# Mixer weights ahead in priority, the mLSTM gate rows and the output gate as later threads: a float32 trunk of two layers

## The chip, the cores and the metric

The kernel runs on one core of a Trainium2 chip. The metric is the device time of one execution in microseconds (us); lower is better.

## The reference

The program is a streaming-encoder trunk with two layers, 512 frames and 1024 channels, all in float32. Each layer adds half a SwiGLU feed-forward block, then a mixer block, then half a SwiGLU block again. The mixer block reads one normalised input through one projection whose columns are shared out among an RWKV-7 mixer, an mLSTM mixer and two merge gates:

```python
xn = _rmsnorm(h, mix_norm[l])
z = xn @ w_in[l]                                  # all columns of both mixers and of the gates
r, k, v, xw, xa, xg = _split_cols(shifted z_rw)   # RWKV-7: 8 heads of 64
...
g = jax.nn.sigmoid(xg) @ g_up                     # RWKV-7's output gate
y_a = ((y + bonus) * g)
y_b = _mlstm_mixer(mq, mk, mv, mo, mi, mf, ...)   # 4 heads of 128, input and forget gate rows mi, mf
u = sigmoid(g_a) * (y_a @ br_a[l]) + sigmoid(g_b) * (y_b @ br_b[l])
h = h + u @ w_out[l]
```

In layer 1 the RWKV value is mixed with that of layer 0 through a low-rank gate (`xn @ vres_down`, then `vres_up`).

## The kernel before, in words

Activations lie transposed, channels on partitions and the 512 frames along the free axis. To keep float32 accuracy every large product is made of three: weights and activations are split into a high part rounded to float32r and a low part that is the rest, and TensorE multiplies high by high, high by low and low by high (`product`, lines 460 to 462). A projection job has 128 output columns and eight steps of 128 input channels, so 24 matmuls. Its weights (512 KB) are loaded by `weights`: one DMA on the SyncE queue into `wraw` (two buffers), then for each half a rounding cast on ScalarE into `whi` (line 424) and a subtraction on VectorE into `wlo` (line 425). `whi` and `wlo` have four half-buffers each, so the splits can be two jobs ahead of TensorE, and no more.

The order of TensorE's work in the mixers is written out by a planner, `Weave`. Each piece of the mixers is a Python generator, a thread with a rank. A thread yields what it waits for: a planned time (`at`), a flag that another thread sets (with a planned time), a lock, or a projection job (`proj`). The planner keeps a planned TensorE time `t` and a planned VectorE time `dve` (`mark`, `pe`); when a thread is ready it runs on, lowest rank first; otherwise TensorE gets the next step of the current job, and a new job goes to the waiting thread of lowest rank. If nobody is ready and nobody waits for a job, the planned time jumps ahead. `manual_schedule` fixes this order for TensorE alone.

The other engines are ordered by the tile framework: each engine's queue is written at build time by going through a planned run and taking, among the instructions that are ready, the one with the lowest priority number. Priority numbers count up in the order in which the program issues instructions. On the chip each queue then runs in that fixed order.

The threads are `common` (rank -1: the jobs `misc`, `wa`, `xg`), four `rwkv` threads (ranks 0 to 3, jobs `k`, `r`, `v` of two heads each, then a chunked recurrence), the mLSTM heads (8), the mLSTM projections (9), the mLSTM gate rows (10) and, as filler, the sixteen merge-gate jobs (`gates_spilled`, 20). Job `misc` carries the mLSTM input and forget gate rows, 32 columns of `xg` and the low-rank value columns. In the kernel before, the gate rows begin when `misc` is shifted (flag `misc`), the jobs follow each other as `misc`, `wa`, `xg`, and `xg` is shifted, passed through a sigmoid and made ready inside `common`, which sets the flag `common`. The RWKV threads begin at the flag `wa`, with the two matmuls of lines 923 and 927 that read `wa`.

Of the kernel before, what the change touches and what calls it, by code (L numbers as in the profile page):

```python
# [12 lines left out]
F32R = mybir.dt.float32r  # L13
AF = mybir.ActivationFunctionType
ALU = mybir.AluOpType
# [215 lines left out]
class Weave:  # L231
# [48 lines left out]
    def run(self):  # L280
        trunk = self.trunk
        job = None
        self.threads.sort(key=lambda th: th[0])
        while job or any(not th[3] for th in self.threads):
            th = next((th for th in self.threads if self.ready(th[2])), None)
            if th is not None:
                if th[2][0] == "lock":
                    self.held.add(th[2][1])
                self.resume(th)
                continue  # L290
            if job is None:
                th = next((th for th in self.threads if th[2][0] == "proj"), None)
                if th is not None:
                    job = [th, trunk.weights(th[2][1]), trunk.mm(), 0]
                    th[2] = ("job", None)
                    self.mark(0.0, 1.4)
            if job is not None:
                th, w, ps, k = job
                trunk.product(ps, w, k, trunk.xh[:, k, :], trunk.xl[:, k, :], k == 0, k == KD - 1)
                self.t += self.STEP + (0.1 if self.small else 0.0)  # L300
                self.small = False
                job[3] += 1
                if job[3] == KD:
                    job = None
                    self.resume(th, ps)
                continue
            times = [th[2][1] for th in self.threads if th[2][0] == "at"]
            times += [self.flags[th[2][1]] for th in self.threads if th[2][0] == "flag" and th[2][1] in self.flags]
            self.t = min(times)
# [19 lines left out]
class Trunk:  # L329
# [246 lines left out]
    def mixers(self, l, done):  # L576
        nc = self.nc
        self.l = l
        self.src = {n: self.a["wi"][l, i] for i, n in enumerate(WIN_TILES)}
        src = self.src  # L580
# [21 lines left out]
        wv.add(-1, self.common())  # L602
        for p in range(4):
            wv.add(p, self.rwkv(p))
        wv.add(8, self.mlstm_heads())
        wv.add(9, self.mlstm_projections())
        wv.add(10, self.mlstm_gates())
# [24 lines left out]
        for i in range(KD):  # L632
            w = self.weights(self.a["br"][l, i])
            for j in (1, 0):
                g = gates[i][j]
                ps = self.mm()
# [23 lines left out]
        self.wv.mark(1.4, 0.7)  # L660

    def gates_spilled(self, early):
        yield "flag", "rows"
        for i in range(16):
            ps = yield "proj", self.src[f"g{'ab'[i % 2]}{i // 2}"]
            g = self.tmp(f"t{1 + i % 2}", 1)
            self.gate(ps, g)
            self.nc.sync.dma_start(out=self.gd[i], in_=g)
            early.add(i)
# [21 lines left out]
    def mlstm_gates(self):  # L691

        nc, l, zm, wv = self.nc, self.l, self.zm, self.wv
        yield "flag", "misc"
        rc, gem = self.tmp("t2", 1), self.m_gem
        slab, rt, ru = self.tmp("t1", 1), self.tmp("t0"), self.tmp("t0")
        ifb = self.col(l, "ifb")
        F = slice(64, 68)
        I = slice(32, 36)
        nc.gpsimd.memset(slab, 0.0)  # L700

        nc.vector.tensor_scalar(out=rt[F], in0=zm[F], scalar1=ifb[F], scalar2=None, op0=ALU.add)
        nc.scalar.activation(out=ru[F], in_=rt[F], func=AF.Abs)
        nc.scalar.activation(out=ru[F], in_=ru[F], func=AF.Exp, scale=-1.0)
        nc.scalar.activation(out=ru[F], in_=ru[F], func=AF.Ln, bias=1.0)
        nc.vector.tensor_scalar(out=rt[F], in0=rt[F], scalar1=-1.0, scalar2=0.0, op0=ALU.mult, op1=ALU.max)
        nc.vector.tensor_tensor(out=rt[F], in0=rt[F], in1=ru[F], op=ALU.add)
        nc.vector.tensor_tensor_scan(out=ru[F], data0=rt[F], data1=rt[F], initial=0.0, op0=ALU.add, op1=ALU.bypass)
        nc.vector.tensor_copy(out=rt[I], in_=ru[F])
        nc.vector.scalar_tensor_tensor(out=slab[I], in0=zm[I], scalar=ifb[I], in1=rt[I], op0=ALU.add, op1=ALU.add)  # L710
        nc.vector.tensor_tensor_scan(out=rc[I], data0=slab[I], data1=slab[I], initial=0.0, op0=ALU.max, op1=ALU.bypass)
        self.split(self.m_rc[I], self.m_rc[F], rc[I])
        nc.vector.tensor_tensor(out=rt[I], in0=rt[I], in1=rc[I], op=ALU.subtract)
        nc.scalar.activation(out=slab[F], in_=rt[I], func=AF.Exp)
        yield "at", wv.mark(16.0, 8.0)
        ps = self.mx()
        self.transposes(ps, [slab[:, P * j : P * j + P] for j in range(4)])
        wv.pe(0.5)
        psv = ps.rearrange("p (j c) -> p j c", j=4)
        nc.vector.tensor_scalar(out=gem[:, :, 0:4], in0=psv[:, :, 32:36], scalar1=-1.0, scalar2=None, op0=ALU.mult)  # L720
        nc.vector.tensor_copy(out=gem[:, :, 4:8], in_=psv[:, :, 64:68])
        wv.set("rows", wv.mark(0.6, 0.6))
# [139 lines left out]
    def common(self):  # L862
# [3 lines left out]
        wv.pe(0.9)  # L866
        self.shifted(ps, "mu_misc", 0, zm)
        rows = wv.mark(7.0, 1.6)
        wv.set("misc", rows)
        ps = yield "proj", src["wa"]  # L870
        self.shifted(ps, "mu_wa", 0, wa)
        nc.scalar.activation(out=wa[0:64], in_=wa[0:64], func=AF.Tanh)
        wv.set("wa", max(rows, wv.mark(4.5, 1.6)))

        yield "at", rows
        ps = self.mx()
        self.transposes(ps, [self.rstd[:, P * j : P * j + P] for j in range(4)])
        wv.pe(0.5)
        nc.vector.tensor_copy(out=self.m_rcol, in_=ps.rearrange("p (j c) -> p j c", j=4)[:, :, 0:1])
        ps = yield "proj", src["xg"]  # L880
        self.shifted(ps, "mu_xg", 0, sg)
        for x in (sg, zm[0:32]):
            nc.scalar.activation(out=x, in_=x, func=AF.Tanh, scale=0.5)
            nc.vector.tensor_scalar(out=x, in0=x, scalar1=0.5, scalar2=0.5, op0=ALU.mult, op1=ALU.add)
        hi = self.sq
        for (lw, lx), R in zip(self.low, (slice(0, 32), slice(96, 128))):
            nc.scalar.copy(out=hi[R], in_=zm[R])
            nc.vector.tensor_tensor(out=lx[32:64], in0=zm[R], in1=hi[R].bitcast(F32), op=ALU.subtract)
            nc.scalar.copy(out=lx[0:32], in_=zm[R])
            nc.scalar.copy(out=lx[64:96], in_=zm[R])  # L890
        wv.set("common", wv.mark(8.0, 3.5))

    def rwkv(self, p):
        wv = self.wv
# [18 lines left out]
    def rwkv_in(self, p):  # L913
# [31 lines left out]
        yield "lock", "halves"  # L945
        self.halve(kk)
        at = wv.mark(5.0, 2.4)
        rz = yield "proj", src[f"r{p}"]
        yield "at", at
        ps = self.sums(0)  # L950
# [12 lines left out]
        nc.vector.scalar_tensor_tensor(out=chunks(a), in0=r, scalar=self.col(l, "r_k", p), in1=chunks(k), op0=ALU.mult, op1=ALU.mult)  # L963
        nc.vector.tensor_tensor(out=r, in0=r, in1=d3, op=ALU.mult)
        self.ready_ar = wv.mark(14.0, 10.5)
        ps = yield "proj", src[f"v{p}"]
        self.shifted(ps, "mu_v", p, v)
        wv.mark(0.0, 1.6)
        if l > 0:
            yield "flag", "common"  # L970
            ps = self.mx()
            lw, lx = self.low[1]
            vg = w
            nc.tensor.matmul(ps, lhsT=lw[:, F], rhs=lx, start=True, stop=True)
            wv.pe(0.25)
            nc.scalar.activation(out=vg, in_=ps, func=AF.Tanh, bias=self.hcol(l, "vb", p), scale=0.5)
            wv.mark(0.0, 2.2)
# [207 lines left out]
    def rwkv_gated(self, p):  # L1185
# [22 lines left out]
        nc.scalar.activation(out=y, in_=y, func=AF.Identity, scale=self.col(l, "gn_w", p), bias=self.col(l, "gn_b", p))  # L1208
        nc.gpsimd.tensor_tensor(out=y, in0=y, in1=chunks(b), op=ALU.add)
        yield "at", wv.mark(6.0, 0.8)  # L1210
        yield "flag", "common"
        ps = self.mx()
        F = slice(P * p, P * p + P)
        nc.tensor.matmul(ps, lhsT=mats[:, 1, F], rhs=sg, start=True, stop=False)
# [58 lines left out]
```

## Time and profile before

| | us |
|---|---|
| median of 3 runs | 2456.25 (2452.19 to 2456.63) |
| the profiled execution's own time | 2451.83 |
| its span, first to last instruction | 2450.1 |
| TensorE busy | 2394.5 |
| VectorE busy | 1306.7 |
| ScalarE busy | 1054.2 |
| GpSimd busy | 111.1 |

The own time of the profiled execution stands at the lower end of the three runs. TensorE's busy time takes the ends of matmuls from a model, so that consecutive matmuls overlap in it; the other engines' times are measured. A name such as L424 is a line of the kernel, `PE` is TensorE, `DVE` VectorE, `ACT` ScalarE, `POOL` GpSimd, `SPq` the SyncE queue that issues the loads. A bracket at the end of a row of the timeline is the engine's idle time ahead of that instruction and what ended it.

### The profile page before, as it was taken

How to read it: one execution, taken by the hardware profiler on the slowest of the kernel's cores; microseconds unless marked ns; L12 is line 12 of the kernel's file. 1: busy time of each engine (PE TensorE's matmuls, PEld its weight loads, DVE VectorE, ACT ScalarE, POOL GpSimd, SP SyncE). 2: the span in 40 equal slices, each digit the busy share in tenths (PEclk: the TensorE clock that was granted, in tenths of full speed). 3: DMA queues.
4: the chain of work that ended last, by engine and by line, in shares of the span. 5: the costliest groups of instructions: out<-in, count | busy, mean ns of one | idle time of the engine just before them, and what ended most of it. 6: DMA issues, size and time to landing. Idle time of an engine off the chain costs nothing.

```text
span 2450.1 us, 33539 instructions
## 1 busy us (share of the span) xinstructions
PE 2394.5 (98%) x13138; PEld 1945.7 (79%) x13138; DVE 1306.7 (53%) x2341; ACT 1054.2 (43%) x1795; POOL 111.1 (5%) x147
## 2 busy tenths in 40 slices
PE   9999998999999999999999999989999999999997
PEld 7888886787787888888888888867777868888886
DVE  5444347776766644444444434487677665444333
ACT  5333336555645443333343333465566454333322
POOL 0000010000000100000000000100000001000012
PEclk9999999999999999999999999999999999999998
DMA  4332342322344422233322323423223444322332
GB/s 157 98 101 95 108 121 85 106 77 84 105 140 146 137 96 95 95 95 101 97 95 95 103 93 112 129 72 101 81 83 105 148 128 134 98 95 95 94 100 82
DMA packets 114751, 256.13 MB, mean 105 GB/s; under 512 B 39808, under 2 KB 43008, under 8 KB 114592
## 3 DMA queue, kind: packets, MB, share of 16 engines
q1 hardware_dynamic: 113968, 252.35, 33.1%
q8 instruction: 103, 1.69, 0.3%
q10 hardware_dynamic: 624, 1.64, 0.2%
q14 instruction: 56, 0.46, 0.1%
HBM read 230.88 MB, written 23.07 MB: 104 GB/s over the span
## 4 chain that ended last, share of the span: by engine, by line
PE 62%; DVE 3%; ACT 2%; DMA 1%; issue 0%; DVEq 0%; POOL 0%; ACTq 0%; SPq 0%; POOLq 0%
PE mm L460 20%; PE mm L462 19%; PE mm L461 19%; DMA yd<-avr 0%; PE mx L673 0%; DMA t<-yd 0%; PE mx L1156 0%; DVE wlo L425 0%; PE mx L781 0%; PE mx L796 0%; DMA t<-mats 0%; PE mx L1144 0%; ACT L512 0%; ACT L513 0%; PE mx L1102 0%
## 5 line engine op out<-in xcount | busy, mean ns | idle before, releaser
L424 ACT CAST whi<-wraw 128x512 fp32r<-128x512 f32 (+1 forms) x800 | 486.1, 610 | 1058.1 <-PE mm L461 1001.9
L460 PE MATMUL mm<-xh,whi 128*128 128x512 f32 x2160 | 862.7, 399 | 11.0 <-ACT whi L424 10.9
L425 DVE TENSOR_TENSOR wlo<-wraw,whi 128x512 fp32r<-128x512 f32 (+1 forms) x800 | 555.8, 697 | 580.9 <-ACT whi L424 573.1
L462 PE MATMUL mm<-xh,wlo 128*128 128x512 f32 x2160 | 845.8, 392 | 4.9 <-DVE wlo L425 4.7
L461 PE MATMUL mm<-xl,whi 128*128 128x512 f32 x2160 | 844.7, 391 | 0.0
L460 PEld LDWEIGHTS mm<-xh,whi 128*128 128x128 f32 x2160 | 407.5, 189 | 105.9 <-ACT whi L424 12.6
L462 PEld LDWEIGHTS mm<-xh,wlo 128*128 128x128 f32 x2160 | 407.3, 189 | 93.6 <-DVE wlo L425 7.2
L461 PEld LDWEIGHTS mm<-xl,whi 128*128 128x128 f32 x2160 | 407.7, 189 | 82.6 <-issue 1.2
L460 PE MATMUL mm<-hh,whi 128*128 128x512 f32 x704 | 273.9, 389 | 0.0
L461 PE MATMUL mm<-hl,whi 128*128 128x512 f32 x704 | 273.9, 389 | 0.0
L462 PE MATMUL mm<-hh,wlo 128*128 128x512 f32 x704 | 273.9, 389 | 0.0
L461 PEld LDWEIGHTS mm<-hl,whi 128*128 128x128 f32 x704 | 132.2, 188 | 27.6
L462 PEld LDWEIGHTS mm<-hh,wlo 128*128 128x128 f32 x704 | 132.2, 188 | 27.5
L460 PEld LDWEIGHTS mm<-hh,whi 128*128 128x128 f32 x704 | 132.2, 188 | 27.2
L539 DVE TENSOR_TENSOR t<-mm,rstd 128x512 f32<-128x512 f32 x88 | 60.9, 692 | 138.7 <-PE mm L462 127.7
L543 DVE TENSOR_TENSOR t<-mm,t 128x512 f32<-128x512 f32 x88 | 60.9, 692 | 130.1 <-PE mm L462 127.8
L508 POOL TENSOR_TENSOR acc<-acc,t 128x512 f32<-128x512 f32 x36 | 47.9, 1330 | 1194.3 <-ACT t L506 1180.1
L541 ACT ACTIVATE t<-t 128x512 f32<-128x512 f32 x88 | 55.8, 634 | 29.4 <-DVE t L539 29.3
L488 DVE TENSOR_TENSOR hl<-t,hh 128x512 fp32r<-128x512 f32 x88 | 61.0, 693 | 9.6 <-ACT hh L487 2.0
L487 ACT CAST hh<-t 128x512 fp32r<-128x512 f32 x88 | 54.7, 622 | 24.6 <-DVE t L543 24.6
L495 ACT ACTIVATE xh<-h,vec 128x512 fp32r<-128x512 f32 x48 | 34.6, 723 | 44.9 <-DVE h L555 33.7
L460 PE MATMUL mm<-yh,whi 128*128 128x512 f32 x128 | 50.5, 400 | 2.5 <-DVE gb L640 1.6
(243 smaller groups left out, 2066.7 us busy)
## 6 DMA issues: line engine op xcount, KB each, us to landing
wraw<-wi SPq DMA_DIRECT2D x94, 512.0 KB, 3.5
wraw<-f2i SPq DMA_DIRECT2D x88, 512.0 KB, 3.3
wraw<-f1i SPq DMA_DIRECT2D x86, 512.0 KB, 3.3
wraw<-f1o SPq DMA_DIRECT2D x32, 512.0 KB, 3.7
wraw<-f2o SPq DMA_DIRECT2D x32, 512.0 KB, 3.5
gd<-t SPq DMA_DIRECT2D x32, 256.0 KB, 4.1
wraw<-br SPq DMA_DIRECT2D x16, 512.0 KB, 3.7
wraw<-wo SPq DMA_DIRECT2D x16, 512.0 KB, 3.3
```

The lines of the kernel that those rows point to most:

```text
L424: nc.scalar.copy(out=hi, in_=raw)
L425: nc.vector.tensor_tensor(out=lo, in0=raw, in1=hi.bitcast(F32), op=ALU.subtract)
L460: nc.tensor.matmul(ps, lhsT=hi, rhs=xh, start=first, stop=False)
L461: nc.tensor.matmul(ps, lhsT=hi, rhs=xl, start=False, stop=False)
L462: nc.tensor.matmul(ps, lhsT=lo, rhs=xh, start=False, stop=last)
L487: nc.scalar.copy(out=hi, in_=x)
L488: nc.vector.tensor_tensor(out=lo, in0=x, in1=hi.bitcast(F32), op=ALU.subtract)
L495: nc.scalar.activation(out=self.xh[:, i, :], in_=h, func=AF.Copy, scale=gain)
L508: eng.tensor_tensor(out=self.acc, in0=self.acc, in1=sq, op=ALU.add)
L539: nc.vector.tensor_tensor(out=g, in0=pg, in1=self.rstd, op=ALU.mult)
L541: nc.scalar.activation(out=s, in_=g, func=AF.Silu)
L543: nc.vector.tensor_tensor(out=p, in0=pu, in1=s, op=ALU.mult)
```

## The change

Inside the planner, a job's weights (the load and the splits) are issued with a priority number that is lower by 150, so that they stand ahead of up to 150 instructions issued before them. The mLSTM gate rows wait for a new flag `first`, set in the first RWKV thread when the element-wise work on its `k` and `r` has been issued, and they use other scratch tiles. `xg` leaves `common` and becomes a thread `output_gate` of rank 4, which also waits for `first`. What is left of `common` after `wa` (the transposes of `rstd` and the low-rank operands) waits for a flag `keys`, set after the first `k` job. The merge-gate filler waits for `wa` and no longer for the gate rows. The flag `common` is split in two, `low` and `sg`.

```diff
-                    job = [th, trunk.weights(th[2][1]), trunk.mm(), 0]
+                    with trunk.tc.high_priority(offset=150):
+                        w = trunk.weights(th[2][1])
+                    job = [th, w, trunk.mm(), 0]
...
+        wv.add(4, self.output_gate())
...
     def gates_spilled(self, early):
-        yield "flag", "rows"
+        yield "flag", "wa"
...
     def mlstm_gates(self):
-        yield "flag", "misc"
-        rc, gem = self.tmp("t2", 1), self.m_gem
-        slab, rt, ru = self.tmp("t1", 1), self.tmp("t0"), self.tmp("t0")
+        yield "flag", "first"
+        rc, gem, slab, rt, ru = self.m_pt[0], self.m_gem, self.m_so, self.m_ee[0], self.m_ee[1]
...
     def common(self):
-        wv.set("misc", rows)
         ps = yield "proj", src["wa"]
         self.shifted(ps, "mu_wa", 0, wa)
         nc.scalar.activation(out=wa[0:64], in_=wa[0:64], func=AF.Tanh)
         wv.set("wa", max(rows, wv.mark(4.5, 1.6)))
-        yield "at", rows
+        yield "flag", "keys"
         ps = self.mx()
         self.transposes(ps, [self.rstd[:, P * j : P * j + P] for j in range(4)])
...
-        ps = yield "proj", src["xg"]
-        self.shifted(ps, "mu_xg", 0, sg)
-        for x in (sg, zm[0:32]):
-            nc.scalar.activation(out=x, in_=x, func=AF.Tanh, scale=0.5)
-            nc.vector.tensor_scalar(out=x, in0=x, scalar1=0.5, scalar2=0.5, op0=ALU.mult, op1=ALU.add)
-        hi = self.sq
+        x = zm[0:32]
+        nc.scalar.activation(out=x, in_=x, func=AF.Tanh, scale=0.5)
+        nc.vector.tensor_scalar(out=x, in0=x, scalar1=0.5, scalar2=0.5, op0=ALU.mult, op1=ALU.add)
+        hi = self.m_ee[1].bitcast(F32R)
...
-        wv.set("common", wv.mark(8.0, 3.5))
+        wv.set("low", wv.mark(4.5, 1.8))
+
+    def output_gate(self):
+        wv, sg = self.wv, self.r_sg
+        yield "flag", "first"
+        ps = yield "proj", self.src["xg"]
+        self.shifted(ps, "mu_xg", 0, sg)
+        self.nc.scalar.activation(out=sg, in_=sg, func=AF.Tanh, scale=0.5)
+        self.nc.vector.tensor_scalar(out=sg, in0=sg, scalar1=0.5, scalar2=0.5, op0=ALU.mult, op1=ALU.add)
+        wv.set("sg", wv.mark(4.0, 2.2))
 
     def rwkv_in(self, p):
         self.halve(kk)
         at = wv.mark(5.0, 2.4)
+        wv.set("keys")
         rz = yield "proj", src[f"r{p}"]
...
         self.ready_ar = wv.mark(14.0, 10.5)
+        wv.set("first")
         ps = yield "proj", src[f"v{p}"]
...
         if l > 0:
-            yield "flag", "common"
+            yield "flag", "low"
...
     def rwkv_gated(self, p):
-        yield "flag", "common"
+        yield "flag", "low"
+        yield "flag", "sg"
```

## Rows read from the trace of the kernel before

**Rows 1.** The page: span, and each engine's busy time, share and instructions.
```profile
span 2450.1 us, 33539 instructions
PE 2394.5 (98%) x13138; PEld 1945.7 (79%) x13138; DVE 1306.7 (53%) x2341; ACT 1054.2 (43%) x1795; POOL 111.1 (5%) x147
```
**Rows 2.** Stretches, middles of both mixers: length, engines' busy time (count), clock, DMA share.
```profile
413.00:770.00 357.00, 349.78 (x2866) 277.59 (x2865) 252.91 (x573) 200.00 (x377) 15.15 (x33) 1.00 0.35 106
1623.00:1970.00 347.00, 339.92 (x2799) 271.86 (x2797) 251.44 (x567) 196.16 (x370) 14.62 (x33) 1.00 0.33 100
```
**Rows 3.** Timeline of TensorE at the front of layer 0's mixers.
```profile
381.18 0.60 PE L673 MATMUL mx<-cst,rstd 128*128 128x128 f32 x4
...
385.62 0.69 PE L923 MATMUL mx<-wa,mats 64*128 64x512 f32 x1 [1.07 <-ACT wa L872]
...
393.30 0.50 PE L460 MATMUL mm<-xh,whi 128*128 128x512 f32 x1 [0.85 <-ACT whi L424]
...
398.56 0.80 PE L462 MATMUL mm<-xh,wlo 128*128 128x512 f32 x1 [4.52 <-DVE wlo L425]
```
**Rows 4.** The same at the front of layer 1's mixers.
```profile
1590.53 0.60 PE L673 MATMUL mx<-cst,rstd 128*128 128x128 f32 x4
...
1593.28 0.39 PE L461 MATMUL mm<-xl,whi 128*128 128x512 f32 x1
1593.51 0.39 PE L462 MATMUL mm<-xh,wlo 128*128 128x512 f32 x1
1596.21 0.69 PE L923 MATMUL mx<-wa,mats 64*128 64x512 f32 x1 [2.31 <-ACT wa L872]
...
1610.45 0.79 PE L460 MATMUL mm<-xh,whi 128*128 128x512 f32 x1 [4.71 <-ACT whi L424]
...
1611.88 0.80 PE L462 MATMUL mm<-xh,wlo 128*128 128x512 f32 x1 [0.21 <-DVE wlo L425]
```
**Rows 5.** Stretches with a granted clock of 0.50 (third number from the end).
```profile
396.40:403.20 6.80, 4.64 (x11) 3.72 (x12) 4.61 (x8) 2.40 (x4) 0.19 (x1) 0.50 0.40 128
...
1608.20:1615.00 6.80, 4.34 (x9) 2.98 (x10) 6.50 (x12) 5.53 (x10) 0.00 (x0) 0.50 0.20 66
1983.70:1987.00 3.30, 3.03 (x6) 1.55 (x6) 1.73 (x3) 2.50 (x4) 0.00 (x0) 0.50 0.38 142
```
**Rows 6.** Timelines of VectorE and ScalarE at layer 0's front.
```profile
381.72 0.48 DVE L702 TENSOR_SCALAR t<-zm,vec 4x512 f32<-4x512 f32 x1
...
383.77 0.75 DVE L574 SCALAR_TENSOR_TENSOR wa<-zt,onemu,wa 128x512 f32<-128x512 f32 x1 [0.46 <-ACT wa L573]
...
384.94 0.62 ACT L872 ACTIVATE wa<-wa 64x512 f32<-64x512 f32 x1
...
386.87 1.28 ACT L705 ACT_TABLE_LOAD   x1
...
392.65 0.60 ACT L424 CAST whi<-wraw 128x512 fp32r<-128x512 f32 x1
...
397.81 0.69 DVE L425 TENSOR_TENSOR wlo<-wraw,whi 128x512 fp32r<-128x512 f32 x1
```
**Rows 7.** Timeline of TensorE at the end of layer 1's mixers.
```profile
1976.67 0.27 PE L1175 MATMUL mx<-st,gt 64*64 64x64 f32 x2 [0.37 <-DVE st L1181]
...
1979.04 0.50 PE L461 MATMUL mm<-yl,whi 128*128 128x512 f32 x1 [0.51 <-DVE yl L488]
...
1983.37 0.59 PE L481 MATMUL mx<-sq,sel 128*128 128x512 f32 x1 [2.46 <-ACT sq L487]
```
**Rows 8.** Groups: count | busy, mean ns | idle before, releaser; then L1181's own durations.
```profile
L424 ACT CAST whi<-wraw 128x512 fp32r<-128x512 f32 (+1 forms) x800 | 486.1, 610 | 1058.1 <-PE mm L461 1001.9
L425 DVE TENSOR_TENSOR wlo<-wraw,whi 128x512 fp32r<-128x512 f32 (+1 forms) x800 | 555.8, 697 | 580.9 <-ACT whi L424 573.1
L1181 DVE TENSOR_SCALAR st<-mx,dc x56: 262/282/286, 532.3 to 1977.0; 128x64 f32<-128x64 f32 x56
```
**Rows 9.** Waits of SyncE's DMA queue: us in total, times, longest.
```profile
SPq L430 <- DVE wlo L425: 1750.2, 370, 22.0
```

## The prediction

> **What bounds the kernel.** I read the page first: TensorE is busy for 98% of the span, VectorE for 53%, ScalarE for 43% [rows 1]. The change adds and removes no matmul, so it can only win TensorE's idle time and its time at half clock. I then asked for stretches, to see where these are. In the middles of the two mixers TensorE idles 357.00 - 349.78 = 7.2 us and 347.00 - 339.92 = 7.1 us, with VectorE at 71% and 72% [rows 2]: little to win there, and a VectorE with some slack but not much. The timeline of TensorE at the two fronts shows the rest. In layer 0 it waits 1.07 us for `wa`, then 0.85 and 4.52 us for the two parts of a weight split: 6.44 us [rows 3]. In layer 1 it waits 2.31, 4.71 and 0.21 us: 7.23 us [rows 4]. [...] The fronts thus lose 6.44 + 7.23 + 2 x 3.4 = 20.5 us. The end of layer 1's mixers is the other place: waits of 0.37, 0.51 and 2.46 us for the last recurrence [rows 7] and 3.3 us at half clock, 1.7 us lost [rows 5]: 5.0 us.
>
> Why are the splits late? The timelines of ScalarE and VectorE tell. The split that TensorE waits for from 393.64 in layer 0 is of job `k0`. Its cast starts at 392.65 and its subtraction only at 397.81 [rows 6], though its buffers are those of `wa` (`xg` took those of `misc`), whose last product was issued before line 673's transposes at 381.18 [rows 3]. In between the two queues work through the gate rows, with a table load of 1.28 us [rows 6], through the low-rank operands, the shift of `xg` and the first RWKV operations. All of these were issued before `k0`'s weights and have lower priority numbers.
>
> **The change, part by part.**
>
> *Front stalls.* The splits get numbers 150 lower, and the gate rows and `xg`'s shift are not there any more: both reasons for the late splits go. `k0`'s buffers are free by the end of `misc`, `r0`'s by the end of `wa`. All four pairs of halves cost 4 x 0.61 us on ScalarE and 4 x 0.70 us on VectorE [rows 8], and half of them fits under `wa`'s own product. I put the split waits (0.85 + 4.52 + 4.71 + 0.21 = 10.3 us) at nothing afterwards. Cover: two jobs of buffers. If the cover fails, one pair late costs 1.3 us.
>
> *A wait is laid bare.* Before, `xg`'s first half covers the time between the end of `wa`'s product and its tanh. After the change nobody waits for a job then: `common` waits for `keys`, `output_gate` and the gate rows for `first`, the filler and the RWKV threads for `wa`. So TensorE stands still until the tanh is through, in both layers. How long? Before, it takes 385.62 - 381.18 = 4.4 us from the end of `wa`'s product to line 923 in layer 0 and 1596.21 - 1590.53 = 5.7 us in layer 1 [rows 3, 4]. What the change takes off this path is line 702 (0.48 us) and the gap between the end of line 574 at 384.52 and the tanh at 384.94, in which other work stood ahead of it (0.42 us) [rows 6]. A split that now goes ahead may put up to 0.6 or 0.7 us back [rows 8]. I take 3.5 us and 4.6 us, 8.1 us in all. Bounds: the times of before, 10.1 us, and the five bare instructions, each near 0.7 us, some 3 us a layer, so 6 us.
>
> *The clock.* It fell behind waits of 4.52 and 4.71 us, and did not fall behind one of 2.31 us [rows 3 to 5]. My 3.5 and 4.6 us lie between these and near the upper. A fall costs 3.4 us as at the fronts or 1.7 us as at 1983.70 [rows 5]. I take 1.7 us a layer, 3.4 us in all; bounds 0 and 6.8 us. Front after: 8.1 + 3.4 = 11.5 us, so the fronts win 20.5 - 11.5 = 9.0 us (from 3.6 to 14.5 us).
>
> *The end of layer 1.* The filler runs out before the last recurrence is through, and TensorE waits for it [rows 7]. The change moves one job (`xg`, 24 matmuls at 0.23 us, the distance of the starts 1593.28 and 1593.51 [rows 4], 5.5 us) and the gate rows' transposes from ahead of the first RWKV pair to behind it. So the recurrence starts that much earlier against the filler, which lasts longer at the end. That could win the whole 5.0 us; I take 3.5 us, because waits in the middle can stretch the chain again. Bounds 0 and 5.0 us. Layer 0 has next to no such tail, and I count nothing for it.
>
> *The mLSTM begins later,* by about four jobs, and filler takes its place. Its ranks 8 to 10 stand behind all RWKV jobs but ahead of the filler, of which there are sixteen jobs, so four of them can change places with it and the last recurrence still ends last; nothing waits for the mLSTM's end. The gate rows themselves (POOL's clearing of `slab`, the scans, the table load) move into a stretch where VectorE is at 71% [rows 2]; no TensorE work needs them soon. Cover gone, their chain costs filler order only. Nothing.
>
> *Splits ahead of chain work.* This is the price. 94 jobs issue 188 casts and 188 subtractions in the mixers, at 0.61 and 0.70 us [rows 8]. Queue order alone moves, not the work, but an operation of the recurrence that TensorE waits for can now find a split ahead of it. The tightest links are the 56 state updates of line 1181 (0.28 us each [rows 8]), each between two matmul groups. Before, they already met a split now and then. I estimate four more hits of 0.70 us that the planner's two steps of cover don't hide: 3 us. Bounds: none (0), and every third update (19 x 0.70 = 13 us); a better order could also win some of the 14.3 us of [rows 2], say 5 us.
>
> [...]
>
> *DMA.* Each weight load is still one DMA of the SyncE queue, moved ahead of the recurrence's small transfers, the `gd` and `yd` stores and the `bonus` reload. That queue already waits 1750.2 us, 370 times, with a load at its head for a buffer that the subtraction frees [rows 9]. Earlier splits free it earlier. I count nothing; if a transfer of the recurrence is held until the load lands, the second rival pays for it.
>
> **Sum.** -9.0 - 3.5 + 3 = -9.5 us. Against the profiled execution's 2451.83 us that is 2442.3 us. That execution lies 4.4 us below the median of the three runs, 2456.25; against the median it is 2446.7 us. I predict **2446 us**, by the median.
>
> **Rivals.**
>
> *First: the bare wait eats the gain.* Both fronts keep the waits of before (10.1 us), the clock falls for the long time in both (6.8 us), the tail wins nothing and chain hits cost the 3 us: 20.5 - 16.9 - 3 = 0.6 us. For it: the waits that I expect are near those behind which the clock fell. Against it: what stood ahead of the tanh does go away. Time 2455.6 us, no difference.
>
> *Second, on the other side: splits hold up the recurrence.* Place: the 56 updates of line 1181 and the operations like them. Each hit costs up to 0.70 us. The front and the tail win 12.5 us, so from 12.5 / 0.70 = 18 hits on, about one update in three, the kernel is slower. With every second update hit (28 x 0.70 = 19.6 us) the time is 2456.25 - 12.5 + 19.6 = 2463 us. For it: VectorE is at 71%, and a split takes twice an update's time. Against it: updates are short and come one after the other, with two product steps planned between them.
>
> *Third: the change doesn't do what it says.* The splits stay late, as buffers and not queue order hold them; then the split waits of 10.3 us and the falls stay, and the wait of 8.1 us takes the place of 3.4 us: 2456.25 + 4.7 = 2461 us. Against it: `k0`'s buffers were free soon after 381.18, and its cast started at 392.65 [rows 3, 6].
>
> **How the numbers follow.** Forecast 0.67; first rival 0.17; second 0.11; third 0.05. The forecast's own range is 2441 to 2452 us: the fronts at 14.5 or 3.6 us, the rest as in the sum. With tail and middle at their best too (14.5 + 5 + 5 = 24.5 us) it is 2432; the first rival ends at 2456. From 2432 to 2458 us I leave out the second and third rivals and a little below. Under 0.2% (4.9 us) a measurement of this kernel can't be told from no change. Faster 0.67, the forecast; same 0.20, the first rival and 0.03 of the third; slower 0.13, the second and the rest of the third.
>
> **What would show it.** In the profile after: line 923 preceded by a wait of 3 to 5 us on the tanh in both layers, no wait for `whi` or `wlo` behind it, the first recurrence's line 481 some 10 us sooner after the norm (5.5 us of it the moved job, the rest regained), the gate rows' table load behind it, fewer waits around the last updates of layer 1, and the same idle time in the middles. Wrong it would be if the clock falls twice in a front, if filler jobs or the recurrence's small groups (lines 1094, 1125, 1175) get waits of their own, or if ScalarE's casts stand waiting for buffers with chain work behind them.

## The result, and the profile after

The changed kernel takes 2487.02 us (median of 4 runs, 2486.54 to 2489.72) against 2456.44 us before: ratio 1.0128, 95% interval 1.0112 to 1.0143, so about 31 us slower. The forecast was 2446 us, with 2432 to 2458 us as its range. The direction is wrong, and the time lies outside the range.

The page of the changed kernel, the lines that answer to [rows 1]:
```profile
span 2488.0 us, 33578 instructions
PE 2414.9 (97%) x13138; PEld 1964.1 (79%) x13138; DVE 1307.1 (53%) x2341; ACT 1059.1 (43%) x1799; POOL 106.7 (4%) x147
```
Of the work that the page counts only ScalarE's differs, by four table loads, and VectorE and ScalarE are about as busy as before. TensorE's busy time has grown by 20 us with the same 13138 matmuls: some of them ran at the lower clock. From 696.5 to 699.7, at a granted clock of 0.50, 128x512 matmuls start 0.43 us apart (698.46 and 698.89), and from 690.0 to 690.8, at 1.00, 0.23 us (690.00 and 690.23).

Waits of TensorE at the fronts, layer 0 and then layer 1 (us in total, times, longest), to be held against [rows 3, 4]:
```profile
PE mx L933 <- ACT wa L875: 4.0, 1, 4.0
PE mx L484 <- ACT sq L490: 2.5, 1, 2.5
...
PE mx L933 <- ACT wa L875: 4.8, 1, 4.8
PE mx L484 <- ACT sq L490: 1.3, 1, 1.3
```
No split is waited for any more, and the bare wait for `wa` has about the size that the prediction gave it. Behind it stand new waits for `sq`.

The gate rows are still in the front, though. Timelines of ScalarE, VectorE and TensorE, layer 0:
```profile
387.32 1.28 ACT L709 ACT_TABLE_LOAD   x1
397.52 0.63 ACT L718 ACTIVATE so<-ee 4x512 f32<-4x512 f32 x1 [0.23 <-DVE ee L717]
...
392.99 1.21 DVE L715 TENSOR_TENSOR_SCAN pt<-so 4x512 f32<-4x512 f32 x1
396.75 0.68 DVE L717 TENSOR_TENSOR ee<-ee,pt 4x512 f32<-4x512 f32 x1
398.07 0.69 DVE L572 TENSOR_TENSOR zt<-mm,rstd 128x512 f32<-128x512 f32 x1
...
393.45 0.39 PE L465 MATMUL mm<-xh,wlo 128*128 128x512 f32 x1
402.25 0.50 PE L484 MATMUL mx<-sq,sel 128*128 128x512 f32 x1 [2.48 <-ACT sq L490]
431.39 0.60 PE L677 MATMUL mx<-cst,so 128*128 128x128 f32 x4
```
Their table load comes at 387.32 us, where it came at 386.87 before [rows 6], and their last ScalarE operation (L718) is through at 398.2. The new flag holds back what the planner orders, TensorE's work; the framework, which orders the other engines by what is ready, still puts the rows in the front. So the rows lay ready for 33 us until TensorE took their transposes at 431.39, and the planner held the mLSTM back for work that was done. Meanwhile the rows stand in the way of the first pair: job `k0`'s product ended at 393.84, and VectorE read it only at 398.07, with the scan (L715), L717 and other operations ahead of it. The wait of 2.48 us for `sq` lies on that path.

Stretches of the changed kernel, the middle of layer 0's mixers as in [rows 2] and the tails' stretches at a granted clock of 0.50, to be held against [rows 5]:
```profile
413.00:770.00 357.00, 342.68 (x2750) 274.81 (x2750) 242.65 (x550) 190.54 (x359) 12.93 (x31) 0.97 0.33 100
...
785.10:795.30 10.20, 7.94 (x17) 4.99 (x16) 5.07 (x9) 7.31 (x11) 0.00 (x0) 0.50 0.49 159
1983.20:2000.30 17.10, 14.59 (x233) 12.57 (x228) 6.41 (x13) 4.59 (x8) 0.00 (x0) 0.50 0.21 72
2007.10:2010.50 3.40, 3.40 (x12) 1.43 (x12) 1.98 (x3) 1.18 (x2) 1.26 (x1) 0.50 0.33 93
2017.30:2024.10 6.80, 6.15 (x15) 4.38 (x14) 3.18 (x5) 3.86 (x6) 0.00 (x0) 0.50 0.71 230
```
The middle's idle time has doubled, 14.3 us against 7.2 us in layer 0. The tails spend 37.5 us at a granted clock of 0.50; before it was the one stretch of 3.3 us in [rows 5].

What TensorE waits for in that middle:
```profile
PE mx L1106 <- ACT u L1101: 7.4, 2, 4.8
PE mx L1137 <- ACT s L1048: 4.7, 4, 2.6
```
Both are results of the recurrence that come through ScalarE. Before, the same stretch has:
```profile
PE mx L1125 <- ACT s L1036: 2.2, 2, 1.8
PE mx L1094 <- ACT u L1089: 0.6, 1, 0.6
```

Three lines by tile and source show the filler's stores (L668 before, L672 after), the mLSTM heads' first product and the gated product. Each has the number of instructions, the durations, and the first and last start. Before:
```profile
L668 SPq DMA_DIRECT2D gd<-t x32: 319/380/1402, 451.7 to 1975.7; - x32
L774 PE MATMUL mx<-rc,sel x8: 395/446/500, 441.2 to 1829.5; 128*128 128x512 f32 x8
L1214 PE MATMUL mx<-sg,mats x16: 590/591/1061, 583.6 to 1986.1; 128*128 128x512 f32 x16
```
After:
```profile
L672 SPq DMA_DIRECT2D gd<-t x32: 319/383/1168, 425.0 to 1982.1; - x32
L778 PE MATMUL mx<-rc,sel x8: 395/436/498, 494.7 to 1891.5; 128*128 128x512 f32 x8
L1227 PE MATMUL mx<-sg,mats x16: 590/592/1220, 591.4 to 2024.4; 128*128 128x512 f32 x16
```
In layer 0 the filler starts 27 us sooner and the mLSTM 54 us later (50 us in layer 1), behind four filler jobs. At the end of layer 1 the last filler store stands 42 us ahead of the last gated product; before, 10 us.

### The profile page after: what moved, and what is told of

The parts are those of the page before. It is cut to its first block, busy times and chain, and to the rows that moved or that the text cites. A ratio compares the mean times of both kernels' runs of the same rounds, so it can differ in the third digit from the quotient of the medians.

```text
span 2488.0 us, 33578 instructions
## 1 busy us (share of the span) xinstructions
PE 2414.9 (97%) x13138; PEld 1964.1 (79%) x13138; DVE 1307.1 (53%) x2341; ACT 1059.1 (43%) x1799; POOL 106.7 (4%) x147
```

## The experiments

The table holds what the stretches of each profiled execution show. Both layers' mixers are added up, from the norm ahead of them to the norm behind. "Front" is the first 45 us, "tail" what lies beyond 370 us. Each entry is idle time (length less TensorE's busy time) / time at a granted clock of 0.50. The expectations write "at 1.2 GHz" for this 0.50; the pages give the clock as a share of full speed, not in GHz. "Fourth pair" is when the last RWKV pair's recurrence begins in layer 0 and 1 (its first product `lhsT=bk`), in us after the norm. "Length" is that of both mixers together. A stretch at 0.50 counts where it begins.
```
kernel               median us  front      middle     tail       fourth pair  length
before               2456.4     13.6/13.6  13.3/3.4    7.7/3.4   313 / 319     984.3
after                2487.0     13.4/13.6  21.8/27.3  16.6/37.5  337 / 340    1021.7
e1 priority only     2457.1      8.9/6.8   17.2/17.0   8.5/3.4   312 / 322     988.8
e2 threads only      2484.7     14.0/20.4  17.0/13.6  16.5/37.5  328 / 341    1014.9
e3 rows early        2462.2      9.4/13.6  17.6/30.8   9.9/6.8   315 / 329     998.6
e4 xg early          2463.0      3.6/3.4   22.0/23.9  13.1/10.2  322 / 324     995.7
e5 both early        2466.3      2.2/0.0   18.7/17.0  13.5/37.5  317 / 344     999.8
e6 rows due          2477.0     13.5/17.0   8.5/3.4   20.8/58.0  332 / 339    1011.5
e9 fill late         2471.0     15.7/17.0  22.0/20.5   6.9/3.4   304 / 320    1001.2
e10 short a          2472.0     10.9/13.6  27.2/23.9   8.1/0.0   325 / 325    1003.9
e11 short b          2466.3     12.6/17.0  24.8/20.4   4.7/0.0   313 / 328     999.2
e12 rows at keys     2485.2     13.4/13.6  14.0/10.2  21.1/58.0  339 / 336    1018.0
e13 prio in front    2446.4      8.3/3.4   12.9/6.8    7.9/3.4   309 / 316     977.2
e14 prio in middle   2462.6     12.2/17.0  18.2/13.6   7.2/10.2  316 / 325     994.6
e15 b, prio front    2463.0     11.7/13.6  22.7/13.6   4.3/0.0   311 / 323     991.4
e16 b, no prio       2463.6     13.6/20.4  22.1/20.4   4.6/0.0   315 / 326     998.0
e17 prio and u       2449.8      8.9/3.4   15.3/6.8    7.5/6.8   309 / 317     979.5
e18 after and u      2477.0     12.8/17.0  13.9/17.0  16.6/34.1  327 / 339    1010.6
```
After the change the mixers idle 17 us more, and TensorE is busy 20 us longer: together the 37 us by which their length has grown between these two executions. None of it lies in the fronts, which are alike.

The theories that the expectations name: **A**, the mLSTM begins late and the filler is spent ahead of it, so that it is missing at the end; **B**, splits stand ahead of the recurrence's operations; **C**, the bare wait at the fronts; **D**, the planner, which always takes the ready thread of lowest rank, finds a worse order of TensorE's jobs.

### Each half of the diff alone

e1, before with only the priority:
```
+with trunk.tc.high_priority(offset=150):
+    w = trunk.weights(th[2][1])
```


> The kernel before with the 150 lower priority of the weight loads and splits alone; all threads as before. Theory A (the threads cost the time: the gate rows wait for the flag `first`, the mLSTM begins some 50 us later, filler jobs are spent ahead of it and are missing later) expects 2435 to 2458 us, no slower than before, and the waits for `whi` and `wlo` at the fronts (4.5 and 4.7 us) gone or down to about 1 us. Theory B (the splits go ahead of operations of the recurrence that TensorE waits for) expects 2472 to 2492 us, with waits of 2 us and more for line 1089's `u` and line 487's `sq`, and clock falls in the middles.

2457.09 us, ratio 1.0007 (0.9998 to 1.0017). e2, the changed kernel without these lines:

> The changed kernel without the lower priority number: the threads alone. Theory A expects 2472 to 2495 us, the first mLSTM head some 50 us later than in the kernel before and at least eight clock falls in the mixers. Theory B expects 2440 to 2462 us and four or five falls.

2484.65 us, ratio 1.0119 (1.0103 to 1.0135). The threads with their flags make the loss. The priority alone seems to do nothing; its table line (front better, middle worse) says that this is a sum of two things.

### Which moved flag

e3: the gate rows wait for `misc` again (the line that sets this flag comes back too).
```
 def mlstm_gates(self):
-    yield "flag", "first"
+    yield "flag", "misc"
```


> The changed kernel with one flag put back: the mLSTM gate rows wait for `misc` again and no longer for `first`. Theory A expects 2445 to 2465 us, because the mLSTM projections begin some 25 us sooner in the planner's order and the filler keeps its place. Theory B, and theory C (the wait for the tanh of `wa`, laid bare at both fronts, is what costs), expect 2478 to 2490 us, as changed.

2462.2 us (1.0011 to 1.003). e4: `output_gate` waits for nothing (its `yield "flag", "first"` goes).

> The changed kernel in which the output gate's thread waits for nothing, so that its job `xg` fills TensorE's wait for the tanh of `wa` as it did before. Theory C expects both waits of 4.0 and 4.8 us ahead of line 933 gone and 2470 to 2480 us. Theories A and B expect at most 5 us less than the changed kernel's 2487, 2482 to 2490 us, since the loss lies behind the fronts.

2462.97 us (1.0017 to 1.0038). e5 has both edits.

> The changed kernel with both threads put back: the gate rows wait for `misc` and the output gate's thread waits for nothing. What stays of the change is the lower priority number, the low-rank operands behind `keys` and the filler behind `wa`. Theory A (the mLSTM begins late and the filler is spent ahead of it) expects both recoveries to add up: 2440 to 2458 us. Theory D (the planner's greedy order has got worse, whatever begins late: its own planned end of the mixers moved from 397.3 and 405.0 to 401.6 and 415.2) goes by the planned ends of this kernel, 396.7 and 420.1, together 14.6 us above those of the kernel before, and expects 2470 to 2488 us.

2466.31 us (1.0029 to 1.0059). e3 falls in A's range; e4 lies below all ranges, and e5 between the two. Either edit gives back 24 us, and both together no more. So the effects don't add, and A as it was put fails in e4 and e5. C can't carry it: e3 gives back as much as e4 with its fronts still at 9.4/13.6, and e5, whose fronts are all but empty, is no faster than e3.

e6 lets the gate rows wait for `first`, but tells the planner that they are due at once, so that the mLSTM's jobs can start early:
```
-yield "at", wv.mark(16.0, 8.0)
+wv.mark(16.0, 8.0)
+yield "at", wv.t
...
-wv.set("rows", wv.mark(0.6, 0.6))
+wv.mark(0.6, 0.6)
+wv.set("rows", wv.t + 0.6)
```


> The changed kernel with one due time changed in the planner: the gate rows are still issued behind `first`, but the planner takes them for done at once, so that the mLSTM projections may begin at 31 and no longer at 65 in planned time. Theory A expects 2450 to 2466 us, as with the gate rows put back. Theory D goes by the planned ends, 413.9 and 418.2, together 29.8 us above those of the kernel before, and expects 2485 to 2505 us.

2477.04 us (1.007 to 1.0104), between both. The mLSTM now starts 73 and 77 us after the norms (66 and 69 before), and the middles idle less (8.5 us), yet the tails are the worse for it. A late mLSTM alone doesn't explain the tails. The third and fourth pairs still start late here.

### The filler itself

e7 and e8 give the changed kernel and the one before more filler. Eight gates of each layer's list are computed and stored a second time:
```
-for i in range(16):
+for i in [*range(16), *range(8, 16)]:
```


> The changed kernel with eight more filler jobs: the merge gates 4 to 7 are computed and stored a second time where TensorE has nothing else to do (planned idle time 9 us and no longer 53 us). If TensorE's idle time and half clock at the end of the mixers are what costs (theory A's filler missing at the end), the falls there go and the time drops to 2465 to 2482 us. If the recurrence's chain itself is late (theory D; planned ends 406.8 and 425.4), the extra jobs win nothing or hold it up: 2485 to 2503 us.

> The kernel before with the same eight more filler jobs, the control of the run above (planned ends 398.1 and 410.1, together 5.9 us later). Both theories expect 2452 to 2466 us.

2525.96 us (1.0272 to 1.0303) and 2482.95 us (1.0097 to 1.0127): both above what any theory gave. The expectations forgot that the planner goes on starting filler until the recurrence's thread ends, past the gap. The profiles have (13402 - 13138) / 24 = 11 and (13282 - 13138) / 24 = 6 more jobs. At an estimated 24 x 0.23 us a job these are 61 and 33 us of work, and they cost 39 and 27 us; so the gaps took in 22 and 6 us. The tails of e7 fall from 16.6/37.5 to 5.4/3.4. There was room for some 22 us of work in the changed kernel's mixers, mostly in the tails.

e9 undoes one line of the diff. The filler waits for the gate rows again:
```
 def gates_spilled(self, early):
-    yield "flag", "wa"
+    yield "flag", "rows"
```


> The changed kernel, with the filler jobs waiting for the gate rows' flag again, as they did before; gate rows and output gate stay late. In the kernel's own plan TensorE then has some 14 us more idle time in each front and little of it ahead of the last recurrence (about 0 and 10 us, where the plan of the changed kernel has 28 and 47). If what costs is filler spent ahead of the mLSTM and missing at the end: the idle time and the time at 1.2 GHz of the tails (16.6 and 37.5 us together after the change) fall to less than half, and the fronts' grow by as much; 2470 to 2490 us. If the end of the last recurrence is late for another reason (other engines' work in its way): the tails stay as they are and the fronts' new idle time comes on top, 2500 to 2525 us.

2471.04 us (1.0057 to 1.0087): 16 us come back with this line (by the ratios 14). The lines of e9 by tile and source:
```profile
L672 SPq DMA_DIRECT2D gd<-t x32: 319/382/1156, 486.3 to 2000.2; - x32
L778 PE MATMUL mx<-rc,sel x8: 390/395/497, 464.2 to 1866.6; 128*128 128x512 f32 x8
L1228 PE MATMUL mx<-sg,mats x16: 590/591/697, 565.8 to 2001.2; 128*128 128x512 f32 x16
```
The last filler store now stands 1 us ahead of the last gated product, not 42. The tails' time at a clock of 0.50 goes from 37.5 to 3.4 us, and the fronts hardly pay, where the expectation had them lose as much. The fourth pair's recurrence (L1014 after, L1015 here; timelines of TensorE) begins 33 us sooner in layer 0:
```profile
711.71 2.05 PE L1014 MATMUL mx<-avr,bk 64*128 64x128 f32 x32
```
```profile
679.02 2.06 PE L1015 MATMUL mx<-avr,bk 64*128 64x128 f32 x32
```
The table's columns go together: each of its layers in which the fourth pair begins later than 330 us after the norm has 10 to 31 us at a clock of 0.50 in its tail, and no other layer has more than 10.2.

What lies ahead of that pair can be counted in the traces. In every run it is about 31 jobs of `common`, the RWKV pairs and the mLSTM; what differs is the filler, by its stores: 7 and 8 jobs before, 9 and 11 after, 11 and 12 in e6, 11 and 11 in e12, 5 and 7 in e9. Each puts an estimated 5.5 us of work ahead of the pair and is missing as cover behind it. From the pair's start to the next norm it takes 177 and 176 us before, and 173 and 172 us after, though two and three jobs fewer are left there. So what the layers grow by, 37 us, is what the pair begins later, 24 + 21 us, less the 8 us saved behind it. By this estimate three jobs make 17 of the 21 us in layer 1. In layer 0 two make 11 of the 24 us; the rest is 8 us more idle time ahead of the pair, mostly the waits for `u` and `s`, and the lower clock.

### Does the planner's own plan tell it?

e10 and e11 take flags for which the plan leaves little time between the last job and the last recurrence; e12 takes one for which it leaves much.
```
 def mlstm_gates(self):
-    yield "flag", "first"
+    yield "flag", "misc"     # e10, e11; "keys" in e12
 def gates_spilled(self, early):
-    yield "flag", "wa"
+    yield "flag", "rows"     # e10; "core0" in e11; as it was in e12
 def common(self):
-    yield "flag", "keys"
+    yield "flag", "first"    # e10 alone
 def output_gate(self):
-    yield "flag", "first"    # e10 alone
```


> The changed kernel with three flags moved: gate rows behind the product of misc, filler behind the gate rows, output gate at once, low-rank operands behind the first pair's operands. In the kernel's own plan the time from the last job's end to the last recurrence's is 12 and 19 us (28 and 47 after the change, 12 and 27 before) and the fronts idle 4.7 us together. If the order of jobs that the planner finds is what set the loss: 2440 to 2456 us, no slower than before. If the split threads themselves cost on ScalarE and VectorE: 2460 to 2475 us, as in the three runs that moved one or both of them back.

> The changed kernel with two flags moved: gate rows behind the product of misc, filler behind the first pair's recurrence; the output gate stays late. Planned time from the last job to the last recurrence 8 and 13 us, planned idle of the fronts 7.8 us each (shared between them: 15.6 us in all). If the plan's order is the cause: 2445 to 2462 us; the tails' time at 1.2 GHz is under 7 us together. If the threads themselves cost: 2462 to 2480 us.

> The changed kernel with the gate rows waiting for the first pair's keys, which come a little sooner than the first pair's operands for which they wait after the change. If a late mLSTM is what costs: a little faster than the changed kernel, 2465 to 2486 us. If it is the order that the planner finds: its plan has 46 and 47 us from the last job to the last recurrence (28 and 47 after the change) and ends 12 us later in layer 0, so 2487 to 2505 us.

2471.99 us (1.0058 to 1.0085), 2466.28 us (1.0037 to 1.0064) and 2485.17 us (1.0106 to 1.0143). The plan foretells the tails: next to nothing at a clock of 0.50 in e10 and e11, 58 us in e12. It does not foretell the time. e10 misses by 16 us, e10 and e11 end in the range of the other theory, that the threads themselves cost, and e12 at the upper end of the range of the late mLSTM, hardly to be told from the changed kernel (ratio 1.0124 against 1.0128); D as I had put it falls. What the short tails win, the middles lose: they idle 25 to 27 us against 13.3 us before.

### The price of the priority

e13 to e16 look for that loss. Jobs planned in the first 40 us of a layer's mixers are told from the others:
```
-job = [th, trunk.weights(th[2][1]), trunk.mm(), 0]
+if self.t < 40.0:            # e14: self.t >= 40.0
+    with trunk.tc.high_priority(offset=150):
+        w = trunk.weights(th[2][1])
+else:
+    w = trunk.weights(th[2][1])
+job = [th, w, trunk.mm(), 0]
```
e13 and e14 put this into the kernel before, e15 into e11's kernel; e16 is e11 without any priority.

> The kernel before, with the splits ahead of other work only for jobs planned in the first 40 us of a layer's mixers. If the priority pays in the fronts and costs in the middles: the fronts' idle time goes from 13.6 to about 9 us and their time at 1.2 GHz from 13.6 to 6.8 us, as in the run with the priority everywhere, and the middles stay as before: 13.6 - 9 + 3.4 = 8 us, so 2447 us (2443 to 2451). If small shifts of order in the middles come out either way and the priority is not their cause: 2452 to 2460 us.

> The kernel before, with the splits ahead of other work only for jobs planned after the first 40 us of a layer's mixers. If splits hold up chain operations in the middles: the price alone, without the fronts' gain, so 8 to 12 us above the kernel before, 2463 to 2468 us, with more time at 1.2 GHz in the middles than before (3.4 us). If not: 2452 to 2459 us.

> The short-tailed kernel with the late output gate (2466 us), with the splits ahead of other work only in the first 40 us of a layer's mixers. If the splits hold up the chain in the middles: 2453 to 2459 us, with the middles' idle time back from 24.8 to about 14 us. If the threads' order does it: 2462 to 2470 us.

> The short-tailed kernel with the late output gate (2466 us), without the priority. If the splits hold up the chain in the middles: 2456 to 2463 us, the middles as before, the fronts with split waits again. If the threads' order does it: 2466 to 2474 us, since only the fronts' gain goes.

e13 takes 2446.38 us (0.9955 to 0.998), faster than both kernels and the fastest of the study. e14 takes 2462.6 us (1.0022 to 1.0047), 0.4 us under its range. The priority pays 7.7 us in the fronts and costs 8.5 us behind them, which cancels in e1. e15 takes 2462.95 us (1.0021 to 1.0044) and e16 2463.6 us (1.0022 to 1.0049). By the ratios each is some 4 us below e11, so the priority has a part in that kernel's loss, but is not what keeps it above the one before: the threads do that, as e15's second expectation has it. e16 falls between its two ranges.

Where the middle's price is paid shows on ScalarE, at the same place of layer 0. e13, where the cast is not ahead:
```profile
665.16 1.28 ACT L959 ACT_TABLE_LOAD   x1
666.46 0.63 ACT L959 ACTIVATE rw_kk<-rw_kk 128x512 f32<-128x512 f32 x1
666.99 0.45 ACT L1094 ACTIVATE u<-mx,cst 64x256 f32<-64x256 f32 x1
667.46 1.28 ACT L960 ACT_TABLE_LOAD   x1
```
e14:
```profile
669.54 0.63 ACT L959 ACTIVATE rw_kk<-rw_kk 128x512 f32<-128x512 f32 x1
671.20 0.62 ACT L429 CAST whi<-wraw 128x512 fp32r<-128x512 f32 x1 [1.03 <-issue]
671.84 1.28 ACT L960 ACT_TABLE_LOAD   x1
673.13 0.63 ACT L960 ACTIVATE rw_kk<-rw_kk 128x512 f32<-128x512 f32 x1
673.66 0.45 ACT L1094 ACTIVATE u<-mx,cst 64x256 f32<-64x256 f32 x1
```
In e13 `u` follows the logarithm (L959) at once, ahead of the table load for the exponential (L960). In e14 the cast of a split comes next, and ScalarE stands idle for 1.03 us ahead of it. The profile names no releaser; TensorE's last product with the high half (L466 at 670.73) ends 0.08 us ahead of the cast, so it very likely stood for its buffer. Then a table load and another operation follow, and only then `u`. On TensorE, e14 and then e13:
```profile
668.58 1.19 PE L1091 MATMUL mx<-xq,mn 16*32 16x16 f32 x64
674.17 1.00 PE L1099 MATMUL mx<-mn,u 32*16 32x16 f32 x64 [2.83 <-ACT u L1094]
...
668.19 0.97 PE L1099 MATMUL mx<-mn,u 32*16 32x16 f32 x64
```
What `u` reads, the product of L1091, had ended at 669.77 in e14, yet ScalarE, idle from 670.17 to 671.20, did not take `u` ahead of the cast. In e13 L1099 has no wait there. The clock fell at 674.6 in e14: 128x512 matmuls start 0.43 us apart behind the wait (676.12 and 676.55), and 0.23 us ahead of it (670.26 and 670.49). So these rows show one cast, 1.03 us of standing, and the table load, L960 and `u` late behind it.

The last two runs put `u` ahead of the splits as well, e17 in e1's kernel, e18 in the changed one:
```
+with self.tc.high_priority(offset=400):
     nc.scalar.activation(out=u, ...)
```


> The run with the priority alone (2457 us), with the ScalarE instruction that writes u put ahead of the splits as well. If splits and table loads ahead of u are the middles' price: the 5.7 us of waits for u fall below 1.5 us, and the middles' time at 1.2 GHz (17 us) with them: 2446 to 2451 us. If other links of the chain are held as well and take its place: 2452 to 2459 us.

> The changed kernel (2487 us), with the ScalarE instruction that writes u put ahead of the splits as well. If the waits for u are what its middles lose: 9.6 us of waits go and some of the 27 us at 1.2 GHz there, so 2470 to 2480 us; the tails stay as they are. If the chain is late for other reasons: 2482 to 2490 us.

2449.76 us (0.9975 to 0.9993) and 2477.01 us (1.0078 to 1.0106): both as the first theory had it. What had held `u` in the changed kernel, on ScalarE ahead of TensorE's wait of 4.77 us at 695.62:
```profile
687.28 0.63 ACT L427 CAST whi<-wraw 128x512 fp32r<-128x512 f32 x1 [0.52 <-PE mm L464]
687.92 1.28 ACT L516 ACT_TABLE_LOAD   x1
...
689.44 1.28 ACT L965 ACT_TABLE_LOAD   x1
690.74 0.63 ACT L965 ACTIVATE rw_kk<-rw_kk 128x512 f32<-128x512 f32 x1
691.39 1.28 ACT L663 ACT_TABLE_LOAD   x1
...
695.10 0.47 ACT L1101 ACTIVATE u<-mx,cst 64x256 f32<-64x256 f32 x1
```
The mLSTM (L516, L663) and a pair's keys (L965) take turns, and each change to or from the logarithm (L965) brings a table load of 1.28 us in these rows. In e18 the waits of the same middle are:
```profile
PE mx L1138 <- ACT s L1048: 4.7, 4, 2.6
PE mx L1107 <- ACT u L1102: 0.9, 1, 0.9
```
`u` is no longer waited for to speak of, `s` as before. The tails stay as they were, so `u` is not what makes them.

e15 and e16 lose in their middles elsewhere. Their waits there, e16, layer 0 and layer 1:
```profile
PE mm L463 <- DVE wlo L426: 2.9, 2, 2.5
...
PE mm L463 <- DVE wlo L426: 4.2, 2, 3.7
```
With the splits not ahead, it is they that come late under this order of jobs: 7.1 us, in e15 as in e16.

## Why the prediction was wrong

**Front stalls and the bare wait: the sizes right, a reason wrong.** No split is waited for, and the wait for `wa` took 4.0 + 4.8 = 8.8 us where 8.1 us was forecast. But I gave as a reason that the gate rows "are not there any more", and had them behind the first recurrence's line 481. They did not leave the front: their table load comes at 387.32 us, ahead of that line's product at 402.25. What I took off the path to the tanh is still there, too: line 706, once 702, at 381.79 us, and two casts of the low-rank operands right ahead of the tanh. That 8.8 us lies near 8.1 us is in part luck. (The wait for the split in layer 0 began at 394.04 us, not at 393.64; nothing hangs on it.)

**"The clock" at the fronts: too small, and a term is missing.** I took one short fall a layer. The clock fell twice in the front of layer 0, as the prediction's signs of being wrong have it (its mean is 0.76 from 384 to 391 us, 1.00 from 391 to 402 and 0.76 from 402 to 409), and the fronts spend 13.6 us at 0.50, as before. The waits for `sq`, 2.5 and 1.3 us, were in no term. The fronts idle 13.4 us after the change and 13.6 us before: the forecast gain of 9.0 us is not there. In e13, where `xg` still covers the wait for `wa`, the priority alone pays 7.7 us: the split part of the term holds, and the bare wait and the waits for `sq` took it back. The price of a fall was also counted too high. No run shows the 3.4 us a fall in the sum of 20.5 us: it was my estimate, half of a stretch of 6.8 us, and takes in idle time that the waits already hold. [rows 5] have TensorE busy for 4.64 and 4.34 us of it, so by the same half an estimated 2.3 and 2.2 us, and the fronts lost some 18 us, not 20.5. What the runs show in its place is 20 us more busy time in both mixers for 58 us more at a clock of 0.50, about a third.

**"The mLSTM begins later ... Nothing": the step that failed, together with "The end of layer 1".** I reasoned that four filler jobs change places with the mLSTM and that the last recurrence still ends last. Four did go ahead of it. What I did not look at is where the last RWKV pair comes in this order. It has two and three filler jobs more ahead of it after the change and begins 24 and 21 us later, and these jobs are missing behind it. The tail of layer 1 should have won 3.5 us; the tails of both layers went from 7.7/3.4 to 16.6/37.5. e9 shows it: the one line that lets the filler go first is worth 16 us. e3, which undoes the late flag of the gate rows alone, gives back 24 us. That jobs behind the first pair leave filler for the end was a right sum of TensorE's work, drawn for the wrong pair: the first pair does begin 6 and 7 us sooner, the fourth does not.

**"Splits ahead of chain work", +3 us: the mechanism right, the place and the size wrong.** e14 measures 8.5 us. It is not mainly the updates of line 1181 at 0.70 us a hit (waits for them grow by 0.5 us in e14), but ScalarE's `u`, where one hit a layer puts a cast that stands and a table load ahead and makes a wait of 2.8 or 2.2 us, with a fall of the clock behind it (128x512 matmuls start 0.43 us apart at 676.12 and at 1692.13). In the changed kernel, with a mLSTM head in the same stretch, it is 4.77 us; e18 puts what `u` costs there at 10 us (9 by the ratios). So the second rival had a share, through another instruction. e2, the threads without the priority, is at 1.0119, though: the priority's gain and price nearly cancel there too, and the rival did not decide the sign.

**The other rivals.** The first, "the bare wait eats the gain", holds in the main for the fronts and says nothing of the 31 us. The third falls: the splits did get early.

**DMA: nothing, as forecast.** No wait of TensorE that was read names a transfer.

**What stays open.** e9 and e18 return 16 and 10 us of the 31 us, each by itself; they were not run together, so that they add is not shown. Nor is it settled which order of the threads would keep e13's gain: e3, e4, e5, e10, e11, e15 and e16 all lie 5 to 17 us above the kernel before, with waits in the middles that move from one link of the chain to another. The gate rows' other scratch tiles were not put back by themselves; e3 keeps them and is 5 us above the kernel before.

## What to carry to other kernels

Where a long chain ends last and filler covers it, ask of every moved job whether it now runs ahead of the last link's operands: that delays the chain and uses up its cover at once, so it is paid at both ends. When a piece of work gets a later flag, look in the trace whether the work itself moved, or only what waits for it. A higher priority should be given only over the stretch where its wait is seen (here the fronts, 2446 us) and not over a whole loop, for an operation put ahead can itself stand and wait, as the cast of e14 did for 1.03 us on ScalarE with `u` behind it. An edit with a gain in one stage and a loss in another measures as nothing (e1): read it by stage before leaving it out.

## What the runs showed of the hardware that was not expected

At 1983.20 to 2000.30 after the change the clock stood at 0.50 for 17.1 us though TensorE was busy for 14.59 us of them; the work there was mostly small matmuls of the recurrence, many of them 32x32 and 64x64, between short waits. So waits of 0.4 to 1.4 us amid such groups went with a longer stretch at 0.50 than the single waits of 4 to 5 us at the fronts did (3.4 to 6.8 us). In both mixers idle time grew by 17 us, the time at 0.50 by 58 us, and TensorE's busy time by 20 us: about a third of the time at 0.50, not the half that the prediction takes.

On ScalarE of the changed kernel each change between the logarithm and the exponential or tanh of two interleaved streams brought a table load of 1.28 us, four of them between 685.16 and 692.68; the exponential at 694.58, behind a tanh, had none. The queue's order, not ScalarE's load of 43%, made the wait of 4.77 us.
